# Row roots sent round through DRAM, query tiles first, small GpSimd steps later, and sample rows sent earlier at the end

## The chip, the core and the metric

The kernel runs on one core of one Trainium2 chip. The core has a matrix engine (TensorE, here PE, with its weight loads PEld), a vector engine (VectorE, DVE), a scalar engine (ScalarE, ACT), a general engine (GpSimd, POOL) and a queue engine (SyncE, SP) that issues most transfers; ACT and POOL issue some too. Each engine works through its own instructions in order and waits on semaphores. The metric is device time in microseconds (us) of one execution, and the median over runs counts.

## The reference

One inference step of a decoder layer for two groups of tokens: a prompt of 512 tokens, and 8 samples of 4 new tokens each (32 rows, with cached keys, values and states). Width is 1024. Cut to what matters:

```
h  = x * rsqrt(mean(x*x) + eps) * norm_mix_pre          # first norm: one root per token
[x_r | q | k | v | g_lru | g_attn] = h @ w_in           # 1024 -> 8 + 8 + 2 + 2 + 8 + 8 column tiles of 128
A  = RG_LRU(causal_conv4(x_r))                          # decay a = exp(-8 * r * softplus(-lambda))
B  = sliding_window_attention(q, k, v, sinks, T5 bias)  # window 128; samples use cached k, v
m  = (sigmoid(g_lru) * (A @ w_lru_o) + sigmoid(g_attn) * (B @ w_attn_o)) @ w_out
x  = x + rmsnorm(m) * norm_mix_post
u  = causal_conv3((rmsnorm(x) * norm_ffn_pre) @ w_up)
y  = x + rmsnorm((gelu(u_gate) * u_val) @ w_down) * norm_ffn_post
```

Outputs are y for both groups and the new states (recurrence, convolutions, key and value windows).

## The kernel before

All matmuls that matter run as three products of split numbers: an activation tile is kept as a high and a low part (hH, hL), a weight tile as wh and wl, and each 128-deep slice takes wh x H, wh x L and wl x H. Activations stand transposed, features on partitions and tokens along the row, in two halves of tokens: 0 to 255, and 256 to 543 (the last 32 are the samples).

**The first norm.** The root of a token belongs to a column of these tiles, so it can't be applied per partition. The kernel multiplies `x` by the gain only (`hsplit`), runs the matmuls on that, and scales the columns of the result afterwards: keys, values, x_r and gates are multiplied by `rep`, a 128 x 544 tile that holds every token's root on all partitions (`scaled`). Queries aren't: `q_done` only splits them, and the root enters the scores as a per-partition factor `rq`. `xrstd` (L417) makes the roots as columns of `ss`: one column per block of 128 tokens, tokens on partitions. `roots` (L539) turns them into `rep`: DVE writes diag(roots) into `dg` (L544), PE multiplies it by a matrix of ones (`ps_rep`, an f32 product of 256 or 288 columns), ACT copies the result to `rep` (L554). This is done for tokens 0 to 255 (`roots(0, 2)`) and later for 256 to 543 (`roots(2, 5)`). The first time, PE also makes the bias table's rows there (`relx` x `ohp`).

**What sets the order.** Through the mixer the order on PE, ACT, DVE and POOL is the order in which the Python code issues it. `step` issues one column tile of one half (24 matmuls, about 3 us) and then calls `tick`, which advances a clock by one, claims and splits coming weights (`wsplit_hi` on ACT, `wsplit_lo` on DVE), and lets every side generator due by then run to its next `yield n` (come again n ticks later). `late` and `last` hold work that is issued one tick later or at a tick's end. `qkv_order` (L236) names the first twelve column tiles: 8 to 15 are queries, 16 and 17 keys, 18 and 19 values. The first five are run over the first half of the tokens, then over the second; the rest take both halves in turn. The products of `step` use three PSUM buffers in turn (`PM`), so a product's buffer must have been read by the third product after it.

**Side work that the change touches.** `params` (L607) turns parameter vectors, and then makes softplus(-lambda) by 24 small instructions on POOL (128 x 8 each, L624 to L636), whose results `cc` and `cneg` the recurrence first needs at tick 60. `attn_tables` and `load_rep` send bias rows through DRAM by POOL's queue (`rscr`, `rrep`, `btab`). `sample_attn(g)` (L876) loads the cached keys in eight pieces, has DVE turn them in 32 x 32 blocks (`kcT`, L893), and goes on a tick or two later.

**The end.** The last down projection runs by token blocks: tokens 0 to 127 (`fg0_*`), then 128 to 255 (`fg1_*`, `tokens`, `ends`); tokens 256 to 543 are finished in the transposed form (`finish_b`), where POOL adds the residual (L1837) and `y_blocks` turns samples into `yb_s` and the first 512 columns of tokens 256 to 383 into `yb_p`. `yb_p` leaves as 16 pieces of 16 KB from SP's queue (`send`), `yb_s` as 4 pieces from POOL's (`samples_out`). The other rows of tokens 256 to 511 are turned by PE and copied by ACT (`rows_t`, `yo`). Here SP's order is the code's too; POOL's is set by a scheduler.

## Time and profile before

| | |
|---|---|
| median of 3 runs | 971.31 us (971.28 to 971.34) |
| the profiled execution | 971.4 us |
| its span, first to last instruction | 969.6 us |
| busy: PE, PEld, DVE, ACT, POOL | 959.3, 951.6, 762.3, 550.3, 166.3 us |
| granted TensorE clock | 1.0 until PE's last work |

The profiled execution is 1.8 us longer than its span (start and end outside the instructions) and 0.1 us above the median. Busy time is the union of an engine's instructions; waits, and the issuing of transfers by SP and ACT, don't count. In a timeline row the first number is the start from the span's start, the second the time from the first instruction's start to the last one's end, "x" the count, and brackets hold the idle time before and what ended it. SPq and ACTq are the issuing of transfers.

### The profile page before, as it was taken

How to read it: one execution, taken by the hardware profiler on the slowest of the kernel's cores; microseconds unless marked ns; L12 is line 12 of the kernel's file. 1: busy time of each engine (PE TensorE's matmuls, PEld its weight loads, DVE VectorE, ACT ScalarE, POOL GpSimd, SP SyncE). 2: the span in 40 equal slices, each digit the busy share in tenths (PEclk: the TensorE clock that was granted, in tenths of full speed). 3: DMA queues.
4: the chain of work that ended last, by engine and by line, in shares of the span. 5: the costliest groups of instructions: out<-in, count | busy, mean ns of one | idle time of the engine just before them, and what ended most of it. 6: DMA issues, size and time to landing. Idle time of an engine off the chain costs nothing.

```text
span 969.6 us, 20080 instructions
## 1 busy us (share of the span) xinstructions
PE 959.3 (99%) x7598; PEld 951.6 (98%) x7598; DVE 762.3 (79%) x1626; ACT 550.3 (57%) x1342; POOL 166.3 (17%) x283
## 2 busy tenths in 40 slices
PE   9999999999999999999999999999999999999997
PEld 8999999999999999999999999999999999999996
DVE  5778888857858555689967878787888888888886
ACT  6544433467476425566867665555556565656642
POOL 2152000003406231230011110101011111111023
PEclk9999999999999999999999999999999999999999
DMA  7885436533334537235147575767667675859543
GB/s 221 235 240 164 149 90 155 157 94 88 92 104 152 172 102 196 66 124 178 46 108 196 132 188 141 183 154 171 166 154 195 143 200 135 203 130 234 178 147 92
DMA packets 247596, 147.26 MB, mean 152 GB/s; under 512 B 36324, under 2 KB 231788, under 8 KB 247468
## 3 DMA queue, kind: packets, MB, share of 16 engines
q1 hardware_dynamic: 237468, 124.15, 43.5%
q0 software_dynamic: 9824, 19.55, 12.0%
q10 hardware_dynamic: 208, 2.30, 0.6%
q8 instruction: 59, 0.97, 0.4%
q14 instruction: 37, 0.30, 0.1%
HBM read 118.21 MB, written 16.74 MB: 139 GB/s over the span
## 4 chain that ended last, share of the span: by engine, by line
PE 92%; DVE 5%; ACT 1%; issue 1%; DMA 0%; DVEq 0%; SPq 0%; POOL 0%; ACTq 0%; POOLq 0%
PE pmin L165 20%; PE pmdn L165 17%; PE pux L1531 16%; PE puy L1531 8%; PE pq L1531 6%; PE pmlo L165 5%; PE pmao L165 5%; PE pmout L165 4%; PE puz L1531 4%; PE pg L165 1%; PE pvp L165 1%; PE psc L165 1%; PE ptok L165 1%; DVE wl_e L168 1%; DMA pt<-pd 0%
## 5 line engine op out<-in xcount | busy, mean ns | idle before, releaser
L165 PE MATMUL pmin<-hH,wh_in 128*128 128x256 f32 (+1 forms) x568 | 163.9, 291 | 0.0
L165 PE MATMUL pmin<-hL,wh_in 128*128 128x256 f32 (+1 forms) x568 | 162.4, 288 | 0.0
L165 PE MATMUL pmin<-hH,wl_in 128*128 128x256 f32 (+1 forms) x568 | 159.1, 288 | 0.0
L165 PE MATMUL pmdn<-fH,wh_dn 128*128 128x256 f32 (+1 forms) x448 | 129.2, 288 | 0.0
L165 PE MATMUL pmdn<-fH,wl_dn 128*128 128x256 f32 (+1 forms) x448 | 128.8, 287 | 0.0
L165 PE MATMUL pmdn<-fL,wh_dn 128*128 128x256 f32 (+1 forms) x448 | 128.7, 287 | 0.0
L165 PEld LDWEIGHTS pmin<-hH,wh_in 128*128 128x128 f32 x568 | 107.2, 189 | 1.4 <-issue 1.2
L165 PEld LDWEIGHTS pmin<-hL,wh_in 128*128 128x128 f32 x568 | 107.2, 189 | 0.1
L165 PEld LDWEIGHTS pmin<-hH,wl_in 128*128 128x128 f32 x568 | 104.7, 188 | 0.2 <-issue 0.2
L177 DVE SCALAR_TENSOR_TENSOR uc<-u,fv,uc 128x560 f32<-128x560 f32 x128 | 101.9, 796 | 1.7 <-ACT uc L1562 1.2
L165 PEld LDWEIGHTS pmdn<-fH,wl_dn 128*128 128x128 f32 x448 | 84.4, 188 | 0.0
L165 PEld LDWEIGHTS pmdn<-fL,wh_dn 128*128 128x128 f32 x448 | 84.3, 188 | 0.1
L165 PEld LDWEIGHTS pmdn<-fH,wh_dn 128*128 128x128 f32 x448 | 84.2, 188 | 0.1
L1659 ACT COPY u<-pux 128x272 f32<-128x272 f32 x52 | 20.1, 386 | 87.2 <-PE pux L1531 87.2
L168 DVE TENSOR_TENSOR u<-puy,u 128x240 f32<-128x240 f32 (+2 forms) x78 | 24.6, 343 | 48.1 <-PE puy L1531 30.5
L174 DVE TENSOR_TENSOR ft<-ft,pmdn 128x256 f32<-128x256 f32 (+1 forms) x104 | 45.0, 433 | 16.6 <-PE pmdn L165 16.4
L283 ACT ACTIVATE wh_in<-raw_in 128x512 fp32r<-128x512 f32 x70 | 42.2, 624 | 21.3 <-issue 12.1
L290 DVE TENSOR_TENSOR wl_in<-raw_in,wh_in 128x512 fp32r<-128x512 f32 x70 | 47.8, 693 | 1.0 <-ACT wh_in L283 1.0
L1562 ACT ACTIVATE uc<-u,fv 128x560 f32<-128x560 f32 x64 | 48.1, 755 | 0.0
L781 ACT ACTIVATE s<-s,st 128x256 f32<-128x256 f32 (+1 forms) x32 | 15.2, 476 | 54.5 <-DVE st L778 43.2
L168 DVE TENSOR_TENSOR wl_dn<-raw_dn,wh_dn 128x512 fp32r<-128x512 f32 x56 | 38.3, 683 | 3.2 <-ACT wh_dn L1480 3.2
L1469 POOL DMA_DIRECT2D raw_up_s<-raw_up_s x26 | 22.0, 848 | 92.6 <-DMA raw_up_s<-raw_up__11280 5.5
(745 smaller groups left out, 3368.7 us busy)
## 6 DMA issues: line engine op xcount, KB each, us to landing
raw_in<-in_w_in_dram SPq DMA_DIRECT2D x35, 512.0 KB
raw_dn<-in_w_down_dram SPq DMA_DIRECT2D x56, 256.0 KB
raw_up_s<-in_w_up_dram SPq DMA_DIRECT2D x25, 512.0 KB
raw_up_s<-raw_up_s POOLq DMA_DIRECT2D x26, 256.0 KB, 4.2
raw_ao<-in_w_attn_o_dram SPq DMA_DIRECT2D x8, 512.0 KB
raw_lo<-in_w_lru_o_dram SPq DMA_DIRECT2D x8, 512.0 KB
raw_out<-in_w_out_dram SPq DMA_DIRECT2D x8, 512.0 KB
pd<-pb SPq DMA_DIRECT2D x12, 256.0 KB
```

Of the source, the lines that this page charges most:

```text
L165: pe.matmul(out, l, r, start=start, stop=stop)
L168: dve.tensor_tensor(out=out, in0=a, in1=b, op=ALU.subtract)
L174: dve.tensor_tensor(out=out, in0=a, in1=b, op=ALU.add)
L177: dve.scalar_tensor_tensor(out=out, in0=a, scalar=s_, in1=b, op0=op0, op1=op1)
L283: act.activation(hl[0], raw, AF.Copy)
L290: (eng or dve).tensor_tensor(out=hl[1], in0=raw, in1=f32(hl[0]), op=ALU.subtract)
L781: act.activation(s3[:, j, :], s3[:, j, :], AF.Exp, bias=ng[:, j:j + 1], accum_out=sm[:, j:j + 1])
L1469: pool.dma_start(out=w["p4"], in_=w["p2"], accum_op=ALU.add)
L1531: pe.matmul(ps[:, :HN], w, x, start=start and k == 0 and i == 0, stop=stop and k == 3 and i == 2, skip_group_check=True)
L1562: act.activation(yt[j][:, 0:FLATU], u[:, 0:FLATU], AF.Copy, scale=fv[:, j:j + 1])
L1659: act.copy(e[nm_], z)
```

## The change

It has four parts. (1) `roots` no longer uses PE and ACT: DVE turns `ss` in 32 x 32 blocks into `ssT` (L547 of the new code), POOL's queue writes each block's column as a row of a DRAM buffer `rrow` (L551), and then reads that row back onto all partitions as `rep` (L553). (2) `qkv_order` starts with three query tiles, so the first key and value tile are fourth and fifth; the special handling of a first key tile goes. (3) The 24 small POOL instructions come 14 ticks after the step before them, not 1; the cached keys of the second group of samples are turned half a tick sooner in the list of due work. (4) At the end, the remaining side work is issued and the samples' rows are sent before the second block's work, and 3 of the 16 pieces of `yb_p` go by POOL's queue.

```diff
--- before.py
+++ after.py
@@ -233,7 +233,7 @@
         c = key[-1]
         return w[:, c * P:(c + 1) * P].rearrange("(k p) n -> p k n", p=P)
 
-    qkv_order = (16, 18, 8, 9, 10, 11, 17, 19, 12, 13, 14, 15)
+    qkv_order = (8, 9, 10, 16, 18, 11, 17, 19, 12, 13, 14, 15)
     order = [("in", c) for c in qkv_order]
     pairs = [("in", z + c) for c in range(8) for z in (28, 0)]
     order += pairs[:13] + [("wg", 0)] + pairs[13:]
@@ -358,9 +358,7 @@
         else:
             mmhalf(ps, key, X, a)
         tick(upto(key, a, look) if target is None else target, 0.5 if quick else 1)
-        if first_:
-            after.append(lambda: mids.insert(1, lambda: done(a, ps)))
-        elif not quick:
+        if not quick:
             (last if len(wunits) <= 2 * FIRST and a == 0 else late).append(lambda: done(a, ps))
 
 
@@ -426,8 +424,10 @@
     h = Full("h")
     for k in range(KD):
         h.alloc(k)
-    ss = cp.tile([P, 4, 5], F32, name="ss")
-    dve.memset(ss, 1.0)
+    ss_ = cp.tile([P, 32], F32, name="ss")
+    ss = ss_[:, 0:20].rearrange("p (z i) -> p z i", z=4)
+    ssT = cp.tile([P, 32], F32, name="ssT")
+    dve.memset(ss_, 1.0)
 
     def xsquare(i, z, on_act):
         n = TOK[i][1]
@@ -534,33 +534,29 @@
 
     ps_ohp = []
 
+    rrow = drp.tile([1, 5 * P], F32, name="rrow")
+
+    def bias_rows():
+        ps = PX("ps_ohp")
+        mm(ps[:NH, 256:256 + WIN], relx, ohp, True, True)
+        ps_ohp.append(ps)
+
     def roots(i0, i1):
-        dg = T(f"dg_{i0}")
         t0 = TOK[i0][0]
-        spans = [(TOK[i][0] - t0, TOK[i][1], i) for i in range(i0, i1)]
-        n = spans[-1][0] + spans[-1][1]
         last.append(lambda: xrstd(i0, i1))
-        for o, w, i in spans:
-            last.append(lambda o=o, w=w, i=i: dve.tensor_scalar(dg[:, o:o + w], ident[:, :w], ss[:, 1, i:i + 1], None,
-                                                                ALU.mult))
-        yield
-
-        def spread_roots():
-            ps = PX(f"ps_rep{i0}")
-            mm(ps[:, 0:n], ones, dg[:, 0:n], True, True)
-            if not i0:
-                mm(ps[:NH, 256:256 + WIN], relx, ohp, True, True)
-                ps_ohp.append(ps)
-            act.copy(rep[:, t0:t0 + n], ps[:, 0:n])
-
-        if i0:
-            spread_roots()
-        else:
-            mids.insert(0, spread_roots)
+        last.append(lambda: dve.transpose(ssT, ss_))
+        columns = ssT.rearrange("(a c) q -> c a q", c=32)
+        for i in range(i0, i1):
+            dst = rrow[0, i * P:(i + 1) * P].rearrange("(a q) -> a q", q=32)
+            last.append(lambda i=i, dst=dst: pool.dma_start(out=dst, in_=columns[5 + i]))
+        end = TOK[i1 - 1][0] + TOK[i1 - 1][1]
+        last.append(lambda: pool.dma_start(out=rep[:, t0:end], in_=rrow[0, t0:end].partition_broadcast(P)))
+        yield
 
     def norms():
         xsquare(0, 1, True)
         yield from roots(0, 2)
+        mids.insert(0, bias_rows)
         yield
         last.extend(lambda k=k: keep_a(k) for k in (0, 4, 1, 5, 2, 6))
         last.append(lambda: xsquares(2))
@@ -620,7 +616,7 @@
         act.activation(la, la, AF.Exp, scale=-1.0)
         dve.tensor_scalar(lz, la, 2.0, None, ALU.add)
         dve.reciprocal(lz, lz)
-        yield
+        yield 14
         pmul = lambda o, x, y: pool.tensor_tensor(out=o, in0=x, in1=y, op=ALU.mult)
         pmul(lz, lz, la)
         pmul(lz2, lz, lz)
@@ -886,7 +882,7 @@
                                   in_=src[a, kv])
         vraw = RAW(f"cache_win_v{g}").rearrange("p (b x) -> p b x", b=4)
         nc.sync.dma_start(out=vraw, in_=I["cache_win_v"][0, 4 * g:4 * g + 4].rearrange("b j k d -> j b (k d)"))
-        yield 2
+        yield 2 - 0.5 * g
         kb4 = kb.rearrange("p (k b x) -> p k b x", k=NKV, b=4)
         for half in range(2):
             kt = S(f"kcT{g}{half}")
@@ -1863,12 +1859,12 @@
             src = yb["p"][:, 0:512].rearrange("p (b c d) -> p b c d", b=4, c=4)
             for a in range(4):
                 for b in range(4):
-                    pieces.append(lambda a=a, b=b: nc.sync.dma_start(out=dst[a, b], in_=src[32 * a:32 * a + 32, b]))
+                    pieces.append(lambda q, a=a, b=b: q.dma_start(out=dst[a, b], in_=src[32 * a:32 * a + 32, b]))
             send(10)
 
-    def send(n):
+    def send(n, q=nc.sync):
         for f in pieces[:n]:
-            f()
+            f(q)
         del pieces[:n]
 
     yo_ = {}
@@ -2009,17 +2005,17 @@
     for f in gains:
         f()
     r0 = rstd(0)
+    while todo or side:
+        slot(0)
+    samples_out()
+    send(3, pool)
     ps = tokens(1, 0)
     yo = [rows_t(3, (0,))]
     tokens_out(0, r0, 0)()
     yo[0]()
-    send(3)
+    send(len(pieces))
     gain = tokens_done(1, 0, ps)
     tokens_out(0, r0, 1)()
-    send(len(pieces))
-    while todo or side:
-        slot(0)
-    samples_out()
     gain()
     fgs[1, 1] = T("fg1_1")[:, 0:512]
     st = SM("nst_t1", [P, 5], "nst_t1")
```

Place 1, PE after the third product's wh matmuls. Before, and then after (`pmin` is the third product, `ps_rep` the spread roots, `ps_ohp` the bias rows):

```order
L165 MATMUL pmin_0_361<-hH_168,wh_in_356 128x256
L165 MATMUL pmin_0_361<-hL_169,wh_in_356 128x256
L165 MATMUL ps_rep_378<-dg_316,ones 128x256
L165 MATMUL ps_rep_378<-ohp,relx 8x128
L165 MATMUL pmin_0_361<-hH_154,wl_in_354 128x256
```

```order
L165 MATMUL pmin_0_368<-hH_168,wh_in_359 128x256
L165 MATMUL pmin_0_368<-hL_169,wh_in_359 128x256
L165 MATMUL ps_ohp<-ohp,relx 8x128
L165 MATMUL pmin_0_368<-hH_154,wl_in_357 128x256
L165 MATMUL pmin_0_368<-hH_156,wl_in_357 128x256
```

The product with `dg` is gone, the bias rows stay. A second one of 288 columns goes in the same way in the second half.

Place 1, POOL at the same time and after. Before, and then after (`rrow` are the roots' rows in DRAM, `rscr`, `rrep` and `btab` the bias table's way):

```order
L658 MEMSET rvec 8x384
L661 DMA rscr<-rvec 8x384
L686 DMA rrep_294<-rscr 128x768
L692 DMA btab_470<-rrep_294 128x2x256
L686 DMA rrep_295<-rscr 128x768
L692 DMA btab_678<-rrep_295 128x2x256
```

```order
L654 MEMSET rvec 8x384
L551 DMA rrow<-ssT 4x32 x2
L553 DMA rep<-rrow 128x256
L657 DMA rscr<-rvec 8x384
L682 DMA rrep_296<-rscr 128x768
L688 DMA btab_471<-rrep_296 128x2x256
L682 DMA rrep_297<-rscr 128x768
L551 DMA rrow<-ssT 4x32 x3
L553 DMA rep<-rrow 128x288
L688 DMA btab_674<-rrep_297 128x2x256
```

The two `rep` transfers each wait for their `rrow` rows to land, with the bias table's transfers behind them.

Place 2, DVE between the two groups of second-half tiles `hL`. Before, and then after (`qL` is a query's low part, `ks` the scaled key, `xn` a kept copy of x):

```order
L514 COPY xn_251<-ps_tb_456 128x288
L514 COPY xn_252<-ps_tb_457 128x288
L168 TENSOR_TENSOR qL_535<-pmin_0_421,qH_534 128x256
L177 SCALAR_TENSOR_TENSOR hL_163<-ps_tb_517,pv,hH_162 128x288
L177 SCALAR_TENSOR_TENSOR hL_165<-ps_tb_518,pv,hH_164 128x288
```

```order
L514 COPY xn_252<-ps_tb_457 128x288
L514 COPY xn_253<-ps_tb_458 128x288
L171 TENSOR_TENSOR ks_0_535<-pmin_0_422,rep 128x256
L177 SCALAR_TENSOR_TENSOR hL_163<-ps_tb_518,pv,hH_162 128x288
L177 SCALAR_TENSOR_TENSOR hL_165<-ps_tb_519,pv,hH_164 128x288
```

The first reader of `rep` now stands here, ahead of four `hL` tiles that PE's second half needs; before, it stood right behind the first product.

Place 3, the end of SP's queue. Before, and then after:

```order
L1979 DMA out_dram<-fg_0_13513 128x512
L1887 DMA out_dram<-yo_13573 128x512
L1866 DMA out_dram<-yb_p 32x4x32 x3
L1979 DMA out_dram<-fg_1_13550 128x512
L1866 DMA out_dram<-yb_p 32x4x32 x3
L1887 DMA out_dram<-yo_13573 128x512
L1979 DMA out_dram<-fg_0_13590 128x512
L1979 DMA out_dram<-fg_1_13605 128x512
```

```order
L1975 DMA out_dram<-fg_0_13512 128x512
L1883 DMA out_dram<-yo_13583 128x512
L1862 DMA out_dram<-yb_p 32x4x32 x3
L1975 DMA out_dram<-fg_1_13549 128x512
L1883 DMA out_dram<-yo_13583 128x512
L1975 DMA out_dram<-fg_0_13600 128x512
L1975 DMA out_dram<-fg_1_13604 128x512
```

Three pieces of `yb_p` are gone from before the last three stores of SP.

Place 3, POOL at the end. Before, and then after (`ft` is the residual sum of one feature tile; DVE turns the last four into `yb_s`):

```order
L1837 TENSOR_TENSOR ft_7493<-ft_7493,x1r_13124 128x288
L1837 TENSOR_TENSOR ft_7623<-ft_7623,x1r_13126 128x288
L1837 TENSOR_TENSOR ft_7725<-ft_7725,x1r_13128 128x288
L1850 DMA out_dram<-yb_s 256x1x32 x4
L2075 UNCONDITIONAL_BRANCH
```

```order
L1833 TENSOR_TENSOR ft_7492<-ft_7492,x1r_13123 128x288
L1862 DMA out_dram<-yb_p 32x4x32
L1833 TENSOR_TENSOR ft_7622<-ft_7622,x1r_13125 128x288
L1862 DMA out_dram<-yb_p 32x4x32
L1833 TENSOR_TENSOR ft_7724<-ft_7724,x1r_13127 128x288
L1862 DMA out_dram<-yb_p 32x4x32
L1846 DMA out_dram<-yb_s 256x1x32 x4
```

The pieces stand between the last sums; and on DVE the four turns of `yb_s` now come before the first block's last multiply-adds (`fg<-fg,nst_t,xtok`), not after them.

## Rows read from the trace of the kernel before

**Rows 1.** The page's part 1, busy time of each engine, share, count

```profile
PE 959.3 (99%) x7598; PEld 951.6 (98%) x7598; DVE 762.3 (79%) x1626; ACT 550.3 (57%) x1342; POOL 166.3 (17%) x283
```

**Rows 2.** Windows: length, busy PE, PEld, DVE, ACT, POOL, clock, DMA share, GB/s

```profile
10.00:15.00 5.00, 4.99 (x40) 4.71 (x39) 4.63 (x15) 3.31 (x8) 2.25 (x4) 1.00 1.04 331
150.00:200.00 50.00, 49.29 (x414) 46.99 (x413) 41.54 (x111) 22.07 (x59) 2.72 (x12) 1.00 0.52 146
```

**Rows 3.** Waits of PE: total us, times, longest

```profile
PE pvp L165 <- ACT tH L834: 0.5, 1, 0.5
```

**Rows 4.** Chain that ended last, first 60 us: start, us, what

```profile
16.87 0.75 PE ps_rep L165 x4
...
33.83 0.48 PE ps_rep L165 x2
...
38.12 3.22 PE pmin L165 x24
```

**Rows 5.** Timeline of PE at the first roots

```profile
16.71 0.59 PE L165 MATMUL ps_rep<-dg,ones 128*128 128x256 f32 x2
17.23 0.39 PE L165 MATMUL ps_rep<-ohp,relx 128*8 128x128 f32 x2
```

**Rows 6.** Timeline of DVE, 14 to 36 us

```profile
14.19 0.48 DVE L544 TENSOR_SCALAR dg<-ident,ss 128x128 f32<-128x128 f32 x2
...
26.16 0.41 DVE L168 TENSOR_TENSOR qL<-pmin,qH 128x256 fp32r<-128x256 f32 x1
27.62 1.79 DVE L177 SCALAR_TENSOR_TENSOR hL<-ps_tb,pv,hH 128x288 fp32r<-128x288 f32 x4 [1.05 <-ACT hH L455]
...
35.30 0.46 DVE L171 TENSOR_TENSOR ks<-pmin,rep 128x288 f32<-128x288 f32 x1 [1.83 <-ACT rep L554]
```

**Rows 7.** Timeline of POOL, 18 to 94 us

```profile
18.98 0.69 POOL L661 DMA_DIRECT2D rscr<-rvec  x1 [6.70 <-DVE rvec L660]
21.33 0.57 POOL L686 DMA_DIRECT2D rrep<-rscr  x1 [1.66 <-DMA rscr<-rvec]
25.81 0.74 POOL L692 DMA_DIRECT2D btab<-rrep  x1 [3.91 <-DMA rrep<-rscr]
...
51.94 0.20 POOL L624 TENSOR_TENSOR lz<-lz,la 128x8 f32<-128x8 f32 x1 [0.78 <-DVE st L174]
...
59.70 0.23 POOL L636 TENSOR_SCALAR cc<-cc 128x8 f32<-128x8 f32 x1
...
93.49 0.10 POOL L952 MEMSET xr<- 128x3 f32 x1 [6.88 <-DVE pb L823]
```

**Rows 8.** Timeline of DVE at the second group's keys

```profile
171.37 1.30 DVE L893 STREAM_TRANSPOSE kcT<-cache_win_k 128x512 f32<-128x512 f32 x2
```

**Rows 9.** Timeline of SP's queue, the last stores

```profile
959.14 0.35 SPq L1979 DMA_DIRECT2D out_dram<-fg  x1
...
961.97 1.41 SPq L1866 DMA_DIRECT2D out_dram<-yb_p  x3
963.48 0.38 SPq L1887 DMA_DIRECT2D out_dram<-yo  x1
963.95 1.41 SPq L1979 DMA_DIRECT2D out_dram<-fg  x2
```

**Rows 10.** Windows of the end, columns as in Rows 2

```profile
960.00:961.50 1.50, 1.50 (x15) 1.50 (x15) 1.47 (x8) 0.89 (x4) 0.00 (x0) 1.00 0.99 360
964.50:968.00 3.50, 0.00 (x0) 0.00 (x0) 0.07 (x1) 0.00 (x0) 0.00 (x0) 0.95 0.91 304
```

**Rows 11.** Timeline of ACT, DVE and POOL at the end

```profile
962.51 1.05 ACT L1885 COPY yo<-pyo 128x512 f32<-128x512 f32 x2
...
957.97 0.35 DVE L177 SCALAR_TENSOR_TENSOR nst_t<-nst_t 128x1 f32<-128x1 f32 x2
...
950.00 6.20 POOL L1837 TENSOR_TENSOR ft<-ft,x1r 128x288 f32<-128x288 f32 x8 [9.42 <-DVE ft L177]
962.17 2.31 POOL L1850 DMA_DIRECT2D out_dram<-yb_s  x4 [5.97 <-DVE fg L171]
```

## The prediction

> **What bounds the kernel now.** I read the page's busy times first: PE works 959.3 of 969.6 us, DVE 79%, POOL 17% [rows 1]. So nearly every gap between PE's first and last matmul is closed, and time can come out of only three things: work that PE itself does, the few waits of PE, and what follows its last matmul. The waits of PE name one between the fill and the end that touches this change, 0.5 us for `pvp` [rows 3]. The chain that ended last shows that PE's two `ps_rep` jobs stand on the path, not beside it [rows 4]. The windows of the end show what follows PE: from 964.5 to 968.0 no engine computes, and the DMA engines move 304 GB/s [rows 10]. Those are the last stores, so the question there is when they could be issued [rows 9]. The profiled execution took 971.4 us and the median is 971.31; my sum is made against 971.4, and 0.1 comes off at the end. About 0.2%, 1.94 us, is what a measurement of this kernel can tell from no change.
>
> **Part 1, the roots leave PE.** The first `ps_rep` begins at 16.71, and the bias rows' product, which stays, begins at 17.23 [rows 5]: 0.52 us goes. The second has 0.48 in the chain [rows 4]. Since PE's matmuls stand back to back, both come off the path: 1.00 us. Bounds: if filling and draining round the shared piece of 0.75 is charged by half, 0.86; if all of it went, 1.23. What DVE and ACT save (two `dg` of 0.48 together, a copy) costs PE nothing now, so I count nothing for it.
>
> **Part 1, the way through DRAM.** The roots must now come in time. The first `dg` starts at 14.19 [rows 6], so the roots exist then. The turn of `ss` is 32 columns; the nearest row is 512 columns in 0.65 (two in 1.30) [rows 8], so between nothing and 0.65, and I take 0.2, since 32 columns are a sixteenth and little besides a fixed part is left. Two `rrow` issues at 0.57 to 0.74 each [rows 7] put the second at about 15. POOL's issue of a transfer and the next one that waits for it stand 2.35 us apart for `rscr` (18.98 to 21.33) and 4.48 for the large `rrep` (21.33 to 25.81) [rows 7]. A row of 128 roots is small like `rscr`: the `rep` transfer goes at 17.3 and lands between 19.7 and 21.8; with both trips long, at 24.
>
> Its first reader is now the key `ks` that stands where `qL` stood at 26.16 [rows 6], some 0.5 earlier with PE: 25.7. So 2 to 6 us of slack. Behind `ks` on DVE stand four `hL` tiles at 27.62 that had 1.05 idle before them [rows 6], and PE's second half uses them: a `rep` that lands after about 27.2 would delay these one for one. The three rows of the second trip start when the later `dg` did, about 33; the last is issued at 34.5, `rep` at 36.9, landing 39.2 to 41.4. Its reader follows the fourth product of the second half, which ended at 38.12 + 3.22 = 41.3 [rows 4], now about 40.3. DVE may wait 1.1 us there; before, it waited 1.83 for the same tile [rows 6], and PE's waits name no product behind it. Cost 0.
>
> The Trainium skill speaks against this way: "DMA: Bandwidth & Descriptors", section "Latency and other measured facts", puts an access to HBM at 0.2 us on average and 2 us at high load, and load is high here (DMA share 1.04 from 10 to 15 us [rows 2]). By that page, as an estimate, each of the two trips could be 2 us longer and `rep` would land at 23.7 to 25.8, at its reader's time; `rscr` and `rrep` in Rows 7 went through DRAM under the tail of the same load and show 2.35 and 4.48.
>
> **Part 2, query tiles first.** A query needs no `rep`, so the first product's buffer is freed by DVE and ACT without the wait for `rep` that a key's `ks` has (1.83 in the second half [rows 6]). The number of PE products is the same, and PE was busy 4.99 of 5.00 us there [rows 2]. The gain is what is left, 0.01 per 5 us; cost and gain 0. The key's and value's own turns on PE come later in the same number.
>
> **Part 3, POOL's small steps and the keys.** The 24 steps run from 51.94 to 59.93 [rows 7], 8.0 us, and move 13 ticks of about 3 us (one product is 3.22 [rows 4]) to about 88 to 96. POOL's next work there, the `xr` memset, had 6.88 idle before it at 93.49 [rows 7]. It may be pushed 2 or 3 us later. POOL is busy 17% [rows 1] and 2.72 us of 150 to 200 [rows 2], so nothing queues up; `cc` is wanted only at tick 60, far behind. 0. The keys' turns (`kcT`, 1.30 us of DVE at 171.37 [rows 8]) move ahead of a softmax block in the same tick. DVE has 41.54 of 50 us busy there [rows 2]. The work before PE's wait for `tH` adds up to the same; so I leave the wait of 0.5 [rows 3]. Bounds: it goes, -0.5; the softmax is late by all of the turns, +1.3.
>
> **Part 4, the end.** SP issues three pieces of `yb_p` from 961.97 for 1.41 us, and only then `yo` at 963.48, at once behind them [rows 9]. ACT copies two `yo` from 962.51 in 1.05 [rows 11], so the first was ready at about 963.1: SP's queue held it 0.4 us. Then come the two `fg` of 963.95 (1.41 for both, the second at about 964.6, behind DVE) and one `yo` from ACT's queue. The four stores of 256 KB plus the samples' rows move in 964.5 to 968.0 at 304 GB/s [rows 10]: 3.50 x 304 = 1064 KB. Unburdened, stores issued at 959.14 and 959.59 [rows 9] moved in 960.0 to 961.5 at 360 GB/s [rows 10]: 0.86 us from issue to data, 1.5 x 360 = 540 KB, two stores, 0.73 each with the rest. Now `yo` goes at 963.1: its data begins at 963.96, and four stores take 2.92, ending at 966.9, against 967.9 to 968.0. Gain 1.0.
>
> Bounds: the last `fg` is not sent before 964.6, and 964.6 + 0.86 + 0.73 = 966.2, which gives 1.75; the smallest is 0.4, if only SP's hold matters and data runs at 304 GB/s as before, or 0 if an end not set by queues stays. The pieces that POOL takes cost it 0.58 each (four in 2.31 [rows 11]). Its sums run from 950.00 for 6.20 us [rows 11]; three issues push the last sum from 956.2 to about 957.9. The turns that make `yb_s` on DVE stand behind `nst_t`, which ends at 958.3 [rows 11], so 0.4 us of cover is left; if it fails, the first block's `fg` wait, the first of which is sent at 959.14 [rows 9], long before the last. Samples' rows leave about 2 us sooner than 962.17 [rows 11] and no longer share the last window.
>
> A rule of the Trainium skill is against those issues between the sums: "GPSIMD Engine Reference", section "1. Specifications", says that GpSimd's SBUF interfaces are shared with VectorE, with contention when DVE has two inputs in SBUF. By it, as an estimate, each issue might be held by one more DVE instruction, 0.65 as for a `kcT`, and the last sum would end at about 959.9, DVE's turns 1.5 us late. Here the eight sums take 0.78 each beside a busy DVE and the issues 0.58 [rows 11], without a held one.
>
> **Sum.** 971.4 - 1.0 (PE) - 1.0 (end) = 969.4; less 0.1, 969.3.
>
> **The rivals.**
> A, the forecast, both gains: 969.3. By the bounds of its terms (0.86 to 1.23 and 0.6 to 1.2), 968.9 to 969.9.
> B, the end doesn't move by more than SP's hold: the last `fg` or the slower rate sets it, gain 0.1 to 0.4. For it: the window moves 304, not 360 GB/s, with its first store long issued. Against it: samples' rows leave that window. 971.3 - 1.0 - 0.2 = 970.1.
> C, PE's wait for `tH` goes too, since the keys' turns are off DVE when it is owed: 969.3 - 0.5 = 968.8, and with 0.2 more at the end 968.6. For it: a turn of 1.30 stands shortly ahead [rows 8]. Against it: it stays in the same tick.
> D, slower: `rep` is late. The first key's DVE job holds four `hL` tiles, and PE loses one for one from 27.2. To be slower than 973.25, it must eat the gains (2.0) and 1.94: landing at 31.1 or later, two trips of 8 us. Against it: the longest trip in Rows 7 is 4.48. For it: DMA share is 1.04 when it starts [rows 2]. 973.5.
> E, what PE saves early is given back before the end, at a place where DVE or a weight's transfer is due by the clock and not by PE: only the end's gain stays, 970.3. Against it: PE's busy share of 99% leaves hardly any such place [rows 1].
>
> **How the numbers follow.** A 0.55, of which 0.34 under 969.37 and 0.21 above; B 0.20; C 0.14; D 0.05; E 0.06. Faster by over 0.2%: 0.34 + 0.14 = 0.48. Same: 0.21 + 0.20 + 0.06 = 0.47. Slower: 0.05. The range goes from 971.3 - 1.23 - 1.75 = 968.3, the bounds of both terms, to 970.8, where PE's gain is halved by waits and the end stays: A, B, C and E lie in it mostly, D not.
>
> **What would show it.** Right: no `ps_rep`, PE's third product continues without a gap, the same job 1.0 us earlier behind 40 us; the first `ks` on DVE waits little or not for a DMA; `pvp` still waits 0.5; the small POOL steps at about 90; `yo` issued at once behind ACT's copy, samples' rows before 962, and the last data about 3.4 us behind that `yo`. Wrong: a long idle of DVE with the `rep` transfer as its releaser and PE waits for `hL` behind it; DVE's `fg` waiting for a late sum on POOL; the last store issued no earlier.

## The result and the profile after

The changed kernel takes 972.73 us (median of 21 runs, 971.69 to 973.85) against 971.36 for the kernel before (21 runs, 970.92 to 971.75): ratio 1.0014, 95% interval 1.0009 to 1.0020. Forecast was 969.3. It is 1.4 us slower, and its runs lie over twice as far apart. The profiled execution is one of 973.3 us, 0.6 above the median, with a span of 971.4.

Where the time went is best seen by PE's lag: the start of the same matmul in the two profiles, after minus before (us).

```
before's time    40     80     98    120    400    420    640    940   end of span
lag           -1.04  -1.01  +0.20  +0.91  +1.24  +1.60  +1.63  +2.04      +1.8
```

The forecast's 1.0 is there at 40 us. It is lost, and 0.9 more, between 80 and 105; another 1.2 goes slowly after 120, of which 0.36 at 415; and the end gives back 0.3, not 1.0.

Of the waits of PE, the changed kernel has these (columns as in [rows 3]; L830 is L834 before):

```profile
PE pmin L165 <- DVE qL L168: 1.1, 2, 0.6
PE pvp L165 <- ACT tH L830: 0.6, 1, 0.6
PE pq L1527 <- DVE b11L L168: 0.4, 1, 0.4
```

The second answers [rows 3] and is as it was. The first and the third are new. PE at the first roots, against [rows 5]:

```profile
16.79 0.39 PE L165 MATMUL ps_ohp<-ohp,relx 128*8 128x128 f32 x2
17.10 0.74 PE L165 MATMUL pmin<-hH,wl_in 128*128 128x256 f32 x4
```

The roots' product is gone. POOL's queue with the two ways through DRAM, against [rows 7]:

```profile
14.63 1.28 POOL L551 DMA_DIRECT2D rrow<-ssT  x2 [2.34 <-DVE ssT L547]
20.18 0.61 POOL L553 DMA_DIRECT2D rep<-rrow  x1 [4.26 <-DMA rrow<-ssT]
...
33.04 1.71 POOL L551 DMA_DIRECT2D rrow<-ssT  x3 [1.94 <-DVE rq L571]
39.33 0.59 POOL L553 DMA_DIRECT2D rep<-rrow  x1 [4.58 <-DMA rrow<-ssT]
```

Of its transfers issued from 33 to 45 us (count, KB each, us to landing):

```profile
rep<-rrow POOLq DMA_DIRECT2D x1, 144.0 KB, 4.8
rrow<-ssT POOLq DMA_DIRECT2D x3, 0.5 KB, 4.7
```

So half a kilobyte takes 4.7 us, and `rep` lands at 39.33 + 4.8 = 44.1. The DMA engines are full there (share 1.11 from 33 to 39 us, 1.10 in the kernel before). The transfer `rscr` of [rows 7], by which the prediction sized these trips, met nearly idle ones and landed in 2.05 us. Here are its window in the kernel before, and those of the first and the second trip's rows in the changed one (columns as in [rows 2], the DMA share last but one):

```profile
18.98:21.03 2.05, 2.05 (x20) 2.05 (x19) 2.05 (x5) 2.05 (x9) 0.69 (x1) 1.00 0.05 9
```

```profile
14.60:19.50 4.90, 4.90 (x41) 4.55 (x41) 3.46 (x8) 4.64 (x14) 1.28 (x2) 1.00 0.75 204
33.04:38.78 5.74, 5.74 (x46) 5.74 (x45) 4.88 (x13) 4.66 (x12) 1.71 (x3) 1.00 1.11 358
```

The rows of the first trip took 4.8 and 4.3 us to land. DVE, against [rows 6]:

```profile
25.20 0.41 DVE L171 TENSOR_TENSOR ks<-pmin,rep 128x256 f32<-128x256 f32 x1
...
44.18 0.46 DVE L171 TENSOR_TENSOR ks<-pmin,rep 128x288 f32<-128x288 f32 x1 [4.18 <-PE pmin L165]
...
54.70 0.28 DVE L727 COPY kout<-pk 128x128 f32<-128x128 f32 x1
56.45 0.69 DVE L168 TENSOR_TENSOR vL<-pv,vH 128x512 fp32r<-128x512 f32 x1 [1.48 <-ACT vH L750]
57.06 0.28 DVE L753 COPY vout<-pv 128x128 f32<-128x128 f32 x1
57.26 0.68 DVE L290 TENSOR_TENSOR wl_in<-raw_in,wh_in 128x512 fp32r<-128x512 f32 x1
...
71.77 0.71 DVE L819 STREAM_TRANSPOSE pb<-s 128x512 f32<-128x512 f32 x1 [1.87 <-DMA pd<-pb]
```

The first `ks` waits for nothing. The second stands 4.18 us; the releaser named, PE's product, ended at 40.3, so it is the other input, `rep`. The turns of the first keys and values (`kout`, `vL`, `vout`), at 45.85 to 46.9 in the kernel before, now come at 54.7 to 57.3, ahead of `wl_in`. At 71.77 the fourth `pb` (the probabilities of one attention block, turned, which SP sends through DRAM as `pd` and reads back as `pt`) waits for an earlier `pd` to leave its buffer. SP's queue in the kernel before, and then in the changed one:

```profile
58.38 0.40 SPq L259 DMA_DIRECT2D raw_in<-in_w_in_dram  x1
61.30 0.34 SPq L826 DMA_DIRECT2D pd<-pb  x1
65.82 1.83 SPq L831 DMA_DIRECT2D pt<-pd  x4
```

```profile
60.01 0.40 SPq L259 DMA_DIRECT2D raw_in<-in_w_in_dram  x1
62.37 0.34 SPq L822 DMA_DIRECT2D pd<-pb  x1
71.72 0.31 SPq L827 DMA_DIRECT2D pt<-pd  x1
```

`pt` can be issued only when `pd` has landed: it goes 4.5 us after `pd` in the kernel before (6.7 in a second profile of it, f0 below), 9.3 now.

The end, SP against [rows 9], and under it DVE and POOL against [rows 11]:

```profile
962.20 0.35 SPq L1975 DMA_DIRECT2D out_dram<-fg  x1
...
964.67 0.68 SPq L1975 DMA_DIRECT2D out_dram<-fg  x1
965.45 0.39 SPq L1883 DMA_DIRECT2D out_dram<-yo  x1
966.39 1.44 SPq L1975 DMA_DIRECT2D out_dram<-fg  x2
```

```profile
957.55 2.61 DVE L171 TENSOR_TENSOR fg<-fr,gpost 128x512 f32<-128x512 f32 x2
...
957.96 0.56 POOL L1862 DMA_DIRECT2D out_dram<-yb_p  x1
958.53 1.07 POOL L1833 TENSOR_TENSOR ft<-ft,x1r 128x288 f32<-128x288 f32 x1
959.56 0.55 POOL L1862 DMA_DIRECT2D out_dram<-yb_p  x1
```

In the kernel before, the same two DVE products took 1.83 us (at 955.51). PE's last work is 2.1 us later here; less that, the first `fg` goes 1.0 us later than before, `yo` at 963.4 (was 963.48), and the last two `fg` 0.3 later.

### The profile page after: what moved, and what is told of

Its sections match the earlier page's. It is cut to its first block, busy times and chain, and to the rows that moved or that the text cites. A ratio compares the mean times of both kernels' runs of the same rounds, so it can differ in the third digit from the quotient of the medians.

```text
span 971.4 us, 20083 instructions
## 1 busy us (share of the span) xinstructions
PE 960.4 (99%) x7594; PEld 952.5 (98%) x7594; DVE 761.9 (78%) x1623; ACT 549.3 (57%) x1340; POOL 172.2 (18%) x293
## 4 chain that ended last, share of the span: by engine, by line
PE 88%; DVE 8%; ACT 2%; issue 1%; DMA 0%; DVEq 0%; ACTq 0%; POOL 0%; POOLq 0%
PE pmin L165 18%; PE pmdn L165 17%; PE pux L1527 16%; PE puy L1527 8%; PE pq L1527 6%; PE pmlo L165 5%; PE pmao L165 5%; PE pmout L165 4%; PE puz L1527 4%; PE pg L165 1%; PE pvp L165 1%; PE psc L165 1%; DVE wl_e L168 1%; DVE wl_in L290 0%; DVE st L772 0%
## 5 line engine op out<-in xcount | busy, mean ns | idle before, releaser
L777 ACT ACTIVATE s<-s,st 128x256 f32<-128x256 f32 (+1 forms) x32 | 15.2, 475 | 57.5 <-DVE st L774 44.1
```

The lines of the kernel that those rows point to most:

```text
L777: act.activation(s3[:, j, :], s3[:, j, :], AF.Exp, bias=ng[:, j:j + 1], accum_out=sm[:, j:j + 1])
```

## The experiments

Medians of 11 runs each, in us, beside the kernel before on the same chip (971.27 to 971.36); intervals are on the ratio. Each reaches about 0.9 us to either side, so a difference of 0.8 between two of these kernels is not clear of it; a trace shows what one run did.

**e0.** No edit: the changed kernel again.

> The changed kernel once more, for its spread and a second trace. Both theories: about 972.7 us, 1.4 above the kernel before (single runs from 971.7 to 973.9). If the slow growth of the lag after 175 us (from +0.96 to +2.07 us, most of it without a wait) belongs to one profiled run and not to the kernel, this trace doesn't show it, and PE's lag at 175 us against the kernel before is again about +0.9 with the transfer pd<-pb issued near 62 us landing after 70 us.

972.65 (971.71 to 974.15), 1.0005 to 1.0023. Its profile, of its fastest run (971.71), loses only 0.43 at 80 to 105 us, but nearly as much after 120 (1.04). `pd` landed by 70.26, and DVE waited 0.2 for it. So the first loss varies by run; the second hardly differs between the two profiles.

**e1.** Small steps at their old tick:

```diff
-        yield 14
+        yield
```

> The changed kernel with the 24 small POOL steps back at their old tick; all else as changed. Theory A (they had held back POOL's 2 MB of transfers, xdram, btab and rrep; moved away, these go ahead of the transfer pd<-pb, which lands 9.3 us after its issue; DVE's next pb waits 1.9 us, its qL come late and PE waits): pd<-pb lands within 6 us, no wait of DVE for it, PE's wait for qL goes, and PE's lag against the kernel before stays near -1.0 us through 100 us: about 970.8 us (-1.9 from 972.7). Theory B (the query tiles first make SP issue a weight's load, raw_in, 1.6 us later at 60 us, and this delays pd<-pb): no change, about 972.7 us, with DVE's wait still near 1.9 us.

971.83 (0.9999 to 1.0016), 0.8 under e0; the two intervals overlap. In the profiled run PE loses 0.00 from 60 to 120 us. POOL's `xdram` and `btab` go 1.4 us later than in e0. But `pd` still lands at 69.93, 7.4 us after its issue: theory A may tip the scale, but it doesn't explain where the slack went.

**e2, e3.** The last hunk of the change undone (e2); the three pieces by SP (e3):

```diff
     # e2: these four lines stand again behind tokens_out(0, r0, 1)(), the pieces as send(3) and send(len(pieces))
-    while todo or side:
-        slot(0)
-    samples_out()
-    send(3, pool)
     # e3
-    send(3, pool)
+    send(3)
```

> The changed kernel with the end of the kernel before (side work and samples' rows after the second block's first part, all pieces of yb_p on SP). Theory A (POOL's issues between its last sums stretch the two DVE products fg<-fr,gpost from 1.83 to 2.61 us, and the yb_s turns ahead of fg cost another 0.4, so that the first fg is sent 1.0 us late and only 0.25 of the end's gain is left): fg<-fr,gpost is back at 1.8 us and the end costs 0.25 us more: about 973.0 us. Theory B (the forecast's end, worth 1.0 us, is there and something else hides it): 973.7 us.

> The changed kernel with the three pieces of yb_p issued by SP at the same point of the program, not by POOL. Theory A (it is POOL's issuing beside DVE that stretches DVE's products): fg<-fr,gpost takes 1.8 us again, the first fg goes 0.8 us sooner, SP's three more issues (1.4 us) find SP idle before it, and the end is 0.4 to 0.8 us shorter: about 972.1 us. Theory B (the stretch comes from something else, the sums or a transfer): fg<-fr,gpost stays near 2.6 us and the time at 972.7 us.

971.89 and 971.90. In both, the two DVE products take 1.83 us again; e3 differs from the changed kernel in who issues, and in that alone:

```profile
956.81 1.83 DVE L171 TENSOR_TENSOR fg<-fr,gpost 128x512 f32<-128x512 f32 x2
```

So the three issues on POOL are the reason, but not by standing beside the products. They push the starts of POOL's last two sums about 0.5 and 1.1 us later, and a sum beside a product is what lengthens it. g1 (below) has the two apart, DVE's products and POOL's work under them:

```profile
955.49 0.68 DVE L171 TENSOR_TENSOR fg<-fr,gpost 128x512 f32<-128x512 f32 x1
956.09 1.43 DVE L171 TENSOR_TENSOR fg<-fr,gpost 128x512 f32<-128x512 f32 x1
```

```profile
955.57 0.57 POOL L1876 DMA_DIRECT2D out_dram<-yb_p  x1 [0.93 <-DVE fr L174]
956.15 0.81 POOL L1847 TENSOR_TENSOR ft<-ft,x1r 128x288 f32<-128x288 f32 x1
```

Beside an issue alone a product takes 0.68 us, as with POOL idle (0.65 to 0.68); beside a whole sum 1.43. In the kernel before and in e3 the last sum covers the first product by 0.7 us, and that one takes 1.23. In the changed kernel sums cover both, 1.39 and 1.30.

That e2 would be slower was wrong: its median is 0.76 lower. e3's shorter products don't show at its end: from PE's last work its span ends 0.1 us sooner than in the kernel before, the changed kernel's 0.3 sooner. Its lower median must come from elsewhere; which part isn't shown.

**f0.** The kernel before, one profile.

> The kernel before, unchanged, for a second trace. All four traces of the changed kernel and its variants lose 1.2 us against the one trace of before between 120 and 940 us, with the same curve (0.36 at 415 us and the rest without a wait). If that belongs to the changed kernel, this trace agrees with the first one of before within 0.1 us all along. If it belongs to that one trace, this one shows the same curve of +0.8 us against it, and only the 0.36 at 415 us is left for the change.

971.21; PE's lag against the first profile of before is within 0.03 us all along. So the slow loss after 120 us belongs to the changed program.

**f1, f2, f3.** State loads 4 ticks later (f1), with the old end (f2), and with eight small DVE memsets at the start (f3):

```diff
-    start_at(14, state_blocks())
+    start_at(18, state_blocks())
     # f3 also, at the start
+    for z in range(8):
+        dve.memset(padt[:, z:z + 1], 0.0)
```

> The changed kernel with the four state loads (st_b<-strow, 2.6 us of SP's queue) started 4 ticks later, so that SP is not busy with them ahead of the load raw_in that went at 60.0 to 60.2 us. Theory B, now with A (the new order of tiles puts the state loads ahead of raw_in, which then shares the DMA engines with POOL's 2 MB, and pd<-pb stands behind it: 4 us of slack are eaten by SP's order, and POOL's earlier transfers eat the rest): raw_in goes near 57.5 us, pd<-pb lands within 6 us of its issue, DVE doesn't wait for it, PE's wait for qL goes and the runs lie closer together: about 971.5 us (0.4 to 1.9 less than 972.7, by run). Theory A alone (POOL's earlier transfers are enough): pd<-pb still lands after 69.9 us and the time stays at 972.7 us.

> As the run with later state loads, and the end of the kernel before. Theory A for the end (the new end gives nothing: POOL's issues stretch DVE's products by 0.8 us, and the yb_s turns ahead of fg make the last fg 0.4 later): 0.5 to 0.8 us less than the run with later state loads and the new end, about 970.8 us. Theory B (the new end is worth its 0.3 to 1.0 us): as much more than that run, 971.8 to 972.5 us.

> As the last, with eight small DVE memsets (128 x 1) more at the program's start, where DVE is idle. Theory: the 0.35 us that DVE stands before the first h2f at 414.9 us, which no semaphore explains and which cost PE 0.36, hangs on the place of that instruction in DVE's stream: shifted by eight instructions, the stop moves elsewhere, and PE's lag at 419 us doesn't grow: 0.3 us less than the run without. Rival (the stop comes from the work itself): it stays at h2f, same time.

971.79, 971.01, 970.93. The idea on SP's order was wrong: with SP free, `raw_in` went later still (62.04 in f1), since it waits for `wl_in` on DVE to free its buffer. What f1's profile shows instead is `ks` at 46.39, DVE idle 6.50 before it, and 2.27 us lost at 80 to 105 without any wait for `pd`. The slow loss after 120 fell from 1.0 and more to 0.30, and PE's wait at 415 was gone; with the memsets it stayed gone. The traces bear out f3's theory all the same: `h2f` is the 832nd DVE instruction recorded, waits counted, in all eight profiles in which DVE stands 0.47 us before it (the changed kernel, e0 to e3, g1, g2, h3), and the 831st, 833rd, 834th or 842nd in the eleven in which it stands 0.11. Why that place costs time isn't shown.

The loss of PE from 60 to 120 us goes with the start of the fourth `pb`, whatever made it late (h4 and h5 come from further down):

```
kernel      ks     4th pb   PE's loss     kernel      ks     4th pb   PE's loss
before     35.30   68.77      -           f3         44.77   71.08     1.16
e1         44.38   70.00     0.00         e3         44.55   71.21     1.33
e0         44.40   70.30     0.43         changed    44.18   71.77     1.92
h5         44.77   70.42     0.27         f2         45.73   71.80     1.96
e2         44.32   70.51     0.87         f1         46.39   72.09     2.27
g3         45.08   70.72     0.98         h4         45.67   71.31     1.61
```

Two regularities explain the table. In all eleven kernels of it that have the second trip, the third `pb` starts 17.44 to 17.46 us after `ks`, and the fourth 8.2 us after the third unless it waits for `pd`. So what `ks` loses beyond 44.2 us passes on in full; what it loses up to there hardly does, for with `ks` at 40.90 (g1) the third `pb` is only 0.25 sooner than in the changed kernel (61.38 against 61.63). And behind the chain PE's lag is the start of the fourth `pb` less 70.9 us (70.84 to 70.96) in all ten that lose; e1, at 70.85, just touches it. In the four kernels with the new order that aren't in the table, g1, g2, h1 and h3, `pb` less PE's lag is 70.1 to 70.6, and PE loses 0.00. So PE follows this chain one for one once it has caught up with it. Which link was late differs: in the changed kernel's profile 61.63 + 8.2 = 69.8 is just in time for a PE 1.0 early, and the 1.9 lost are the wait for `pd`; in f1 the 2.27 are all `ks`. `pt` goes 6.9 to 9.4 us behind this `pd` in all fifteen profiles with the new order, 4.5 to 6.7 in the four with the old.

**g1, g2.** The second roots by PE and ACT as before, the first through DRAM (g1), with the old end (g2):

```diff
-        yield from roots(2, 5)
+        yield from roots_on_pe(2, 5)    # dg, ps_rep and act.copy as in the kernel before
```

> The changed kernel, but the second roots (tokens 256 to 543) go to rep by PE and ACT as in the kernel before; the first stay on the way through DRAM. Theory C (the second trip lands at 44.2 to 46.4 us, not at 39 to 41 as forecast; DVE stands 4.2 to 6.5 us before ks, and this eats the slack of the attention chain, so that the fourth turn pb comes after 70.0 us and PE loses about 1.1 us for each us beyond: 70.0 gave 0.0, 70.5 0.9, 71.2 1.3, 71.8 1.9, 72.1 2.3): ks starts by 41.5 us, the fourth pb by 69.5, PE loses nothing from 60 to 120 us, the runs lie within 0.6 us of each other, and PE pays 0.48 for ps_rep: about 971.9 us, with none above 972.5. Theory A (POOL's earlier transfers are enough by themselves to delay pd<-pb): the fourth pb still waits for pd<-pb beyond 70 us and the time is 972.7 + 0.5 = 973.2 us.

> As the last, with the end of the kernel before. Two pairs so far gave 0.76 and 0.78 us for the old end: about 971.1 us, a little under the kernel before (first ps_rep gone: 0.5 us). If the end's difference came from something else in those pairs, the same as the last run.

971.84 and 971.63. In g1's profile, of its fastest run (971.15), `ks` is in time (40.90) and PE loses 0.00, though it pays 0.48. But the fourth `pb` is no sooner than 70.12, since `pd` lands at 70.08:

```profile
70.12 0.71 DVE L833 STREAM_TRANSPOSE pb<-s 128x512 f32<-128x512 f32 x1 [0.47 <-DMA pd<-pb]
```

PE is at -0.5 there and not at -1.0, so it meets the chain half a microsecond later. Single runs still reach 973.3, where none above 972.5 was expected; what those lost isn't shown.

**g3.** The second roots through DRAM by SP's queue, old end:

```diff
-        yield from roots(2, 5)
+        yield from roots(2, 5, nc.sync)
```

> The changed kernel with the old end, and the second roots through DRAM by SP's queue and not by POOL's (rrow and rep). Theory C with POOL's queue as the slow part (rrow's last issue to rep's issue 5.1 us, landing 4.9 us later): by SP the issues cost 0.4 to 0.5 each and each trip about 2 us, rep lands by 40 to 41 us, ks starts at its product's end at 40.5, nothing is lost from 60 to 120 us, and both ps_rep are saved: about 970.4 us. Rival (the trip is slow because the DMA engines are full with the weights' loads of 36 to 40 us, whichever queue sends it): rep still lands at 43 us or later, and SP, which stands waiting for rrow, sends its next weight late: 971 us or more.

971.58. `rep` goes at 39.27, as by POOL, and `ks` starts at 45.08 with the transfer named as releaser:

```profile
45.08 0.46 DVE L171 TENSOR_TENSOR ks<-pmin,rep 128x288 f32<-128x288 f32 x1 [3.26 <-DMA rep<-rrow]
```

The rival holds for the trip as a whole. Its parts differ: SP, held by its weight loads, sends the three rows only at 34.11 to 36.23; the last lands within 3.0 us (4.6 by POOL), and `rep` then takes up to 5.8 (4.8).

**g4.** The kernel before with the last hunk of the change alone, and the two hunks that let `send` take a queue:

```diff
+    send(3, pool)    # ahead of tokens(1, 0), with the side work and samples_out()
```

> The kernel before with nothing changed but the end (side work and samples' rows first, three pieces of yb_p by POOL). Theory A for the end (POOL's issues stretch two products of DVE from 1.83 to 2.6 us and the yb_s turns stand ahead of fg): slower than before by 0.3 to 0.8 us, about 971.9 us. The forecast: 970.3 us.

971.14 (0.9988 to 1.0005): 0.2 less than before, though the two DVE products take 2.58. Neither theory's size was right.

**h1, h2.** The kernel before with the order alone (h1; the special handling of a first key tile goes with it), with the steps alone (h2):

```diff
-    qkv_order = (16, 18, 8, 9, 10, 11, 17, 19, 12, 13, 14, 15)
+    qkv_order = (8, 9, 10, 16, 18, 11, 17, 19, 12, 13, 14, 15)
     # h2, ahead of the small steps
-        yield
+        yield 14
```

> The kernel before with nothing changed but the order of the first column tiles (three query tiles first, and no special handling of a first key tile); roots by PE, old steps, old end. Theory D (the order by itself moves the turns of k and v to the time of the attention blocks: DVE's wl_in goes at 57 us and not at 55.5, raw_in 1.6 us later, pd<-pb lands at 69 to 71 us, and the 0.36 at 415 us and the slow 0.7 come with the order too): about 972.2 us, PE's lag +1.0 at the end. Theory C (the second trip through DRAM is what delays the chain): pd<-pb lands by 68 us, no lag before 400 us, and the time is 971.4 us, or 972.0 if the later 0.36 and 0.7 come with the order.

> The kernel before with nothing changed but the 24 small POOL steps 13 ticks later. Theory A (they held POOL's transfers back; now these go at 47 to 56 us, 3 to 8 us sooner): in this order the weights' load raw_in at 58.4 and pd<-pb at 61.3 come after them, and pd<-pb lands by 66 us or sooner: no wait, 971.4 us. Rival (sooner transfers delay an earlier pd<-pb or pt<-pd): 0.5 us slower or more.

h1 takes 971.80 (971.37 to 972.02; ratio 0.9996 to 1.0014), 0.49 more; with the roots on PE `pd` lands at 70.57 all the same:

```profile
70.61 0.71 DVE L821 STREAM_TRANSPOSE pb<-s 128x512 f32<-128x512 f32 x1 [0.36 <-DMA pd<-pb]
```

So the late chain comes with the order. It costs PE nothing at 80 to 105 here, where PE is 0.1 late and not 1.0 early; with PE 1.0 early the same `pb` would cost 70.6 - 70.9 + 1.0 = 0.7, an estimate. 0.3 of the slow loss comes with the order. h2 takes 971.27, the same as before.

**h3, h4, h5.** The edits of g1 and e1 (h3); of e1, f1 and e2 (h4); of e1 and f1 (h5):

```diff
-        yield 14
+        yield                              # h3, h4, h5
-    start_at(14, state_blocks())
+    start_at(18, state_blocks())           # h4, h5
```

> The changed kernel with the second roots on PE and the small steps at their old tick. If the second trip and POOL's earlier transfers both feed the delay, neither is left: the fourth pb by 69.5 us, all runs within 0.6 us, about 971.5 us (PE -0.5, later 0.36 and 0.7 as in the changed kernel). If the order alone is enough, pd<-pb lands at 70 us again and the runs spread over 1.5 us or more: 971.8 us.

> Roots through DRAM and query tiles first as changed; small steps at their old tick, state loads 4 ticks later, old end. With state loads later the slow growth after 120 us was 0.3 and not 1.2 us; with the steps back the loss at 80 to 105 us was 0.0. Both together: PE's lag -1.0 at 60 us, at most 0.3 lost by 120 us, and -0.4 at the end: about 970.6 us, 0.7 under the kernel before. If ks, which waits for rep, alone decides, 1 us is lost at 80 to 105 us as before and the time is 971.0 us.

> The last run's h4 kernel (970.18 us) with the new end in place of the old one. If the end's worth is what the kernel before showed (0.2 us off): 970.0 us. If the first two pairs were right (0.77 us for the old end): 970.9 us. In either case fg<-fr,gpost takes 2.6 us for two again, against 1.83.

h3: 971.51, the fourth `pb` at 69.63, loss 0.00, ten of eleven runs within 0.8. h4: 970.18 (969.56 to 971.29), ratio 0.9989 (0.9981 to 0.9998): 1.1 under the kernel before and 2.5 under the changed one, the fastest of all. Its profile fell on its second slowest run (971.05), which lost 1.61, so most of its runs probably lose less. h5: 970.84.

The old end thus gave 0.76, 0.78, 0.21 and 0.66 in four pairs of the changed kind, and lost 0.22 in the kernel before. The traces show two sizes of it. With the old end POOL sends the samples' rows either at once behind the last `yb_s` turn, as in e2, or some 1.1 us later, as in h1 (and in before, g2, g3, h2):

```profile
961.71 2.29 POOL L1846 DMA_DIRECT2D out_dram<-yb_s  x4 [4.88 <-DVE yb_s L1852]
```

```profile
962.54 2.30 POOL L1848 DMA_DIRECT2D out_dram<-yb_s  x4 [5.98 <-DVE fg L171]
```

From PE's last work the span ends 0.9 us sooner in e2, f2, f3 and h4 than in before; not in g2 and g3 (0.1 and 0.3; f0, the same kernel as before, has 0.1). With the new end it is 0.2 to 0.3 in the changed kernel, e0, e1, f1, g1 and h5, so the traces don't explain the 0.21 between g1 and g2. In the late programs POOL goes 0.05 to 0.09 us after the end of a later DVE product (the first `fg<-pend`) and 1.4 after the last turn of `yb_s`, so it waits for more than its own tiles; why there and not in the others wasn't found.

## Why the prediction was wrong, point by point

Three prices failed: the order of the tiles and the second trip, both at 0, which together cost PE 1.9 us in the profiled run, and the end at 1.0, which gave 0.3.

- **PE's work**: right. 1.0 us less by 40 us in the changed kernel, 0.5 in g1 with one product left.
- **Roots through DRAM, first trip**: right in effect, too short in size. `rep` went at 20.18, not 17.3, and landed at 24.0, the end named for two long trips; `ks`, at 25.20, didn't wait.
- **Second trip, priced 0**: the step that failed first. It was sized by `rscr` (2.35) and set to land at 39.2 to 41.4 with a wait of at most 1.1; by POOL's queue it landed at 44.1 to 46.3 and DVE stood 4.2 to 6.5 us. That takes all the slack ahead of the third `pb`, and what goes beyond delays PE (f1). The prediction has `rscr` "under the tail of the same load"; it met the DMA engines at 0.05, and the trip falls where they are at 1.11. The Trainium skill's rule that was set aside ("DMA: Bandwidth & Descriptors", section "Latency and other measured facts") would have added 2 us to each of the two trips, as an estimate, and so 43.2 to 45.4; the trace agrees with that better than with the sum.
- **Query tiles first, priced 0**: failed. Only PE's products and the wait for `rep` were counted, not where the keys' and values' later jobs land on DVE. They moved from 46 to 55 us, in front of `wl_in`; that delays `raw_in`, and `pd` behind it, for which the fourth `pb` waits 1.87. Alone the order takes 0.49 more (h1), none of it at the chain by its trace: it uses up the slack that PE's gain then needs.
- **Small steps, priced 0**: right alone (h2), in doubt with the rest: POOL's transfers went 1.8 us sooner, beside `raw_in` and `pd`; taking that back goes with 0.8 less (e1), within the intervals. "Nothing queues up" was read from POOL, not from the DMA engines they share. The steps ran from 89.7 to 97.6 (13 ticks of 3 us from 51.94 make 91, not 88).
- **Rival E** named what happened, that PE's gain is given back at a chain that doesn't move with it. It had 0.06, on the ground that PE was 99% busy; that shows that there was no wait, not how near one was. And it counted only the gain as lost: behind the chain PE's lag is whatever the chain's is, 0.9 us in the profiled run.
- **Keys turned sooner**: right, PE's wait for `tH` is 0.6, was 0.5.
- **The end, 1.0 forecast**: 0.3 by the trace, 0.2 alone (g4). `yo` left SP's queue only 0.1 us sooner, because the first `fg` was 1.0 later and all behind it too. POOL's last sum was sized well (957.9; it ended at 959.6, less PE's lag 957.5). What was left out is that it then stands beside the DVE products that lead to `fg`; only the turns of `yb_s` were asked for cover. The rule of the Trainium skill on interfaces shared by GpSimd and VectorE ("GPSIMD Engine Reference", section "1. Specifications") was set aside on the row of POOL's sums; it should have been weighed on DVE's side. The trace agrees with it: the DVE product with two inputs takes 0.68 us without and 1.43 beside a sum of POOL (g1), and a sum that starts under such a product takes 1.07 in place of 0.78.
- **Not in the prediction**: 1.0 to 1.2 us lost after 120 in the changed kernel and e0 to e3, 0.5 in g1, g2 and h3, 0.2 to 0.3 in f1 to f3, g3, h1, h4 and h5, 0.0 in f0, g4 and h2. In the changed kernel, e0 to e3, g1, g2 and h3, 0.36 of it is DVE standing before the first `h2f` at 415 with no semaphore outstanding, which goes with that instruction's place among DVE's. The rest has no wait. Its cause stays open.

In the sum of the profiled run: -1.0 + 1.9 + 1.2 - 0.3 = +1.8, the difference of the spans. Against the forecast of -2.0 the chain makes half of the miss, the slow loss a third, the end the rest.

## What to carry to other kernels

On an engine that is 99% busy, ask of each chain that feeds it how late it may come; moving work off the engine takes from that slack, and so does every reordering of the engines beside it. Size a small transfer by a row that went when the DMA engines were as busy as they will be then: `rscr`'s 2.05 us were taken at a share of 0.05, the rows' 4.3 to 4.8 at 0.75 and 1.11. When one engine's work moves in time, ask what stands beside it on the other engines then. When the order of tiles changes, follow the jobs that come ticks behind each tile, and the buffers and loads that wait for them.

## What the runs showed of the hardware

From POOL's queue to landing, 12 KB took 2.05 us with the DMA engines at a share of 0.05; half a kilobyte took 4.3 to 4.8 at 0.75 and 4.6 to 4.7 at 1.11. By SP's queue half a kilobyte landed within 3.0 us of its issue at 1.03, but `rep` could be issued no sooner (39.27 against 39.33), since SP sent the rows later. A DVE product with two inputs took 0.68 us beside POOL's issue of a transfer, as with POOL idle, and 1.23 to 1.43 beside POOL's sums. And between two programs with the same products on PE after 120 us the lag can grow by 0.8 us in 800 with no wait shown, alike in the two profiles of the changed kernel and with nothing of it between the two of the kernel before.
